# Another formula for the booked time of a TensorE product, in the planner that places the side work of a two-layer block

## The chip, the cores and the metric

The kernel runs on one core of a Trainium2 chip. A core has TensorE (matrix products, PE in the profile, with its weight loads as PEld), VectorE (DVE), ScalarE (ACT), GpSimd (POOL) and the queue engine SyncE (SP). Each engine runs its instructions in the order in which the program lists them and waits where an input or a buffer is not ready. The metric is the time of one execution on the device, in microseconds.

## The reference

Two layers, each on 256 latent tokens `x` and 256 context tokens `ctx` of width 1024. Cut to what matters:

```
h = rmsnorm(x, norm_w) * (1 + scale) + shift          # scale, shift, gate from w_ada; the same for ctx
parts = split_cols(h @ w_in)                          # 13 parts, 13328 columns
A: h_a = mlstm(q, k, v, gates), 4 heads, two directions; context first, then x
   y_a = rmsnorm(h_a) * sigmoid(o) * silu(z)
B: differential attention, 8 heads with two maps each; q and k normalised over 64 features, rotated
   y_b = rmsnorm(o_b) * (1 - lam_init) * silu(z)
C: y_c = real(fft2(u)) * silu(z), 4 groups of 256 features
y = sum over A, B, C of sigmoid(m) * (y_i @ w_i_out)
x = x + gate * (y @ w_out)                            # ctx likewise, except in the last layer
```

All values are 32-bit floats. The result is `x` after both layers.

## The kernel before

Every matrix product of two 32-bit operands is made of three TensorE products of a rounded part and its remainder (`hi*hi`, `hi*lo`, `lo*hi`; `three` in the code). The normalised input stands feature-major in `hTh` (rounded) and `hTl` (remainder), 8 blocks of 128 features by 512 tokens.

The main stream goes through the columns of all weights in pieces of 512 rows by 256 columns (272 where the gate columns of branch A ride along). For each piece SyncE's queue loads `raw` (4 buffers), ScalarE casts it to `wh` and VectorE subtracts to get `wl` (3 buffers each), and TensorE multiplies. `next_piece` asks `prefetch` to emit these steps three pieces ahead. A chunk of 256 columns uses two pieces; its result stands in one of three PSUM banks `pm` and is drained by ScalarE and VectorE. The order of the chunks is a list per layer: `A0 A1 ... W0` (heads of A, pairs of heads of B, groups of C, merges M, output W).

All else is side work, written as generators: the gates of branch A (`gates_side`), the scores and weighted sums of a head of A (`a_side`), the softmax of B, the transforms of C, the columns of `w_ada`, and the norm of the next layer (`next_norm`, four units, each four transposes on TensorE, two `ntmp` on ScalarE, two on VectorE, the cast `hTh` on ScalarE and the remainder `hTl` on VectorE). They use five further PSUM banks `ps`. Between two main products `tick` lets the side generators take a step. When a step is due is decided by the planner while the program is written: `Clocks` keeps an estimated time for each engine, every instruction adds a booked duration to its engine's clock (`mm` and `transpose` for TensorE, `Paced` for the others), and starts no earlier than the booked ends of what it reads. A generator yields the time at which its next step may go, mostly `when(...)`: the booked end of its inputs plus 400 ns. `tick` takes the step once TensorE's clock has passed that time, at most 500 ns of TensorE's work at once, and only while the clocks of VectorE and ScalarE are less than 1500 ns ahead of TensorE's (4000 in W). The whole order on every engine comes out of these booked numbers.

Names for what follows. In branch A, `acol` and `ecol` hold per-token gate values, `dR` gate values in memory; `a_side` loads them back, spread over 128 partitions, as `Rb` (a DMA that GpSimd issues, 448 KB in layer 1), forms four score blocks, copies them to `S`, runs four `Rb` relus with `acol` and an exponential, and multiplies. `to` and `Ga` are the output gates of a head. `vt`, `qkh`, `Q`, `K`, `sq`, `bst` belong to branch B: `bst` are sums of squares (VectorE), raised to a power by GpSimd (two instructions each). In the second layer the first head of A does its gates first and then finishes whatever is left of the norm units:

```
            if l and h == 0:
                yield from oz()
                drain(normers)
```

The functions that book TensorE's time and what takes the steps:

Of the kernel before, what the change touches and what calls it, by code (L numbers as in the profile page):

```python
# [10 lines left out]
F32 = mybir.dt.float32  # L11
# [39 lines left out]
def a_parts(d, stream):  # L51
    """(source token tile, first query token, queries, offset) of each position of direction d"""
    o = S_ORDER[d]
    if stream == 0:
        return [(o[0], 0, 256, 0), (o[1], 128 * o[1], 128, 256)]
    return [(o[0], 256, 256, 0), (o[1], 256, 256, 256), (o[2], 256, 256, 512), (o[3], 128 * o[3], 128, 768)]
# [34 lines left out]
class Clocks:  # L91
    """When each engine gets to what is emitted, estimated, to place the side work among the main products."""

# [4 lines left out]
    def book(self, engine, outs, ins, cost, tail):  # L98
        """an instruction of engine: names of tiles written and read, time held, time until the result is seen"""
        start = self.t[engine]  # L100
        for n in outs + ins:
            e, at = self.wrote.get(n, (engine, 0.0))
            if e != engine:
                start = max(start, at)
        for n in outs:
            for e, at in self.read.get(n, {}).items():
                if e != engine:
                    start = max(start, at)
        self.t[engine] = end = start + cost
        for n in ins:  # L110
            self.read.setdefault(n, {})[engine] = end + SEM_NS
        for n in outs:
            self.wrote[n] = (engine, end + tail + SEM_NS)
        return end

    def rotate(self, tag, bufs, name):
        """the tile called name takes the place of the one bufs before it"""
        r = self.ring.setdefault(tag, [])
        r.append(name)
        if len(r) > bufs:  # L120
            self.read[name] = {"": self.last(r[-1 - bufs])}
# [5 lines left out]
class Paced:  # L127
    """An engine whose instructions are booked as they are emitted."""

# [37 lines left out]
def hybrid_kernel(ctx: ExitStack, tc: tile.TileContext, t):  # L167
    nc = tc.nc
    x_in, ctx_in, out = t["x"], t["ctx"], t["out"]
    est = Clocks()  # L170
# [15 lines left out]
    def when(*tiles, banks=1):  # L186
        """the time at which the tiles are written and side banks are free"""
        r = est.ring.get("ps", [])
        old = r[-SIDEB:][:banks] if len(r) >= SIDEB else []
        return max([0.0] + [est.wrote[v.name][1] for v in tiles if v.name in est.wrote] + [est.last(n) for n in old]) + READY_NS  # L190
# [14 lines left out]
    def gen_pair(shape, name):  # L205
        """hi and lo parts, in one slot where they fit"""
        if 8 * int(np.prod(shape[1:])) <= 4128:
            p = gen([shape[0], 2] + shape[1:], F32R, name)
            return p[:, 0], p[:, 1]
        return gen(shape, F32R, name), gen(shape, F32R, name)  # L210
# [17 lines left out]
    def mm(o, a, b, start, stop):  # L228
        n = int(np.prod(b.shape[1:]))
        ins = [v.name for v in (a, b) if v.name not in ("hTh", "hTl")]  # L230
        est.book("pe", [o.name], ins, max(n * 0.4167 + 2.5, 27) * (4 if b.dtype == F32 else 1) / (128 // o.shape[0]), 160)
        nc.tensor.matmul(out=o, lhsT=a, rhs=b, start=start, stop=stop)  # L232

    def transpose(o, a, idn):
        est.book("pe", [o.name], [a.name], 112, 160)
        nc.tensor.transpose(o, a, idn)  # L236
# [8 lines left out]

    # ------------------------------------------------------------- constants
    xt = {}
# [72 lines left out]
    def rstd_of(ss, n, shape):  # L320
        """(ss / n + eps) ** -0.5 on GpSimd, in place; returns the time at which it is done"""
        gpsimd.tensor_scalar(ss, ss, 1.0 / n, EPS, op0=ALU.mult, op1=ALU.add)
        gpsimd.tensor_tensor(ss, ss, chalf.to_broadcast(shape), op=ALU.pow)
        return when(ss)

    # ------------------------------------------------------------- per-layer small parameters
    def load_params(l):
# [35 lines left out]

    # ------------------------------------------------------------- adaLN
    def ada_bias(l, piece):
        """b_ada of 1024 columns in the first two rows of a tile of zeros"""
        brow = gen([128, 1024], F32, "brow")
        gpsimd.memset(brow, 0.0)
        gpsimd.dma_start(out=brow[0:2, :],
                            in_=t["b_ada"][l:l + 1, 512 * piece:512 * piece + 1024].to_broadcast([2, 1024]))  # L370
        return brow

    def ada_rows(l, piece, dma):
        """w_ada of 512 columns"""
        raws = []
# [7 lines left out]
    def ada_mm(raws, brow, dst):  # L383
        """sc @ w_ada + b_ada: partitions 32 g + stream hold four partial sums"""
        ps = ps_side()
        for k in range(KT):
            g = k % 4
# [10 lines left out]
    def ada_finish(l, pc, ks=slice(0, 8)):  # L398
        """pc: shift and scale of some blocks of features"""
        if l not in abt:  # L400
# [8 lines left out]
    def ada_gen(l, pieces):  # L409
        """shift and scale columns (pieces 0..3) as a side generator"""  # L410
        acc = small([128, 32], "adac", 1)
# [32 lines left out]

    # ------------------------------------------------------------- norm -> feature-major h
    hTh = const.tile([128, KT, 512], F32R, tag="hTh", name="hTh")
    hTl = const.tile([128, KT, 512], F32R, tag="hTl", name="hTl")

    def norm_stats(tiles):
        """normalized copies of some token tiles"""  # L450
        outs, sums = [], []
# [9 lines left out]
    def norm_apply(l, i, src, base):  # L461
        """src: the normalized transposed blocks base .. base + 3 of token tile i; returns the closing step"""
        ab = abt[l]
# [21 lines left out]

    # ------------------------------------------------------------- weight pieces
    plan = []
# [57 lines left out]
    def wcols(w, *cols, form=None):  # L545
        """two pieces of some columns; even features before odd ones along the columns or in pairs of row blocks"""
        srcs = [(w[:, c:c + n], n) for c, n in cols]
        plan.append((0, srcs, form))
        plan.append((1, srcs, form))

    # ------------------------------------------------------------- main-stream products
    def three(o, a, b, first, last):
# [8 lines left out]
    def fm_chunk(rhs, evac, ntok, bank=ps_main, step=4):  # L561
        """two 128-column blocks of W, feature-major: out[block][128 cols, tokens]"""
        if isinstance(ntok, int):
# [23 lines left out]
    def tm_chunk(lhs, tiles, evac, single=False, step=4):  # L587
        """256 columns of W, token-major: out[pair][128 tokens, 2, 256]"""
        n = 1 if single else 2
# [22 lines left out]

    # ------------------------------------------------------------- side machinery
    side = []
# [38 lines left out]

    # ============================================================= one layer
    def layer(l, P):
# [8 lines left out]
        def packed(name, i):  # L664
            """[128, 2, NTOK], two of them in a slot where they fit"""
            if NTOK == 512:
# [4 lines left out]

        # ---------- branch A: gates
        def gates_side():
            """kind x head i of the gate preactivations: from column 32 x + i, token-major, to a partition"""
            yield when(gpad)
# [69 lines left out]

        # ---------- branch A: heads
        def a_proj(h):
# [178 lines left out]

        # ---------- branch B
        def b_proj(g):
# [57 lines left out]
        def b_side(g):  # L986
# [37 lines left out]
            def softmax(hd, i, p2, n):  # L1024
                """the weighted difference of both maps, short of the first one's 1 / sum"""
                c0 = 4 * i + 2 * hd
# [89 lines left out]

        # ---------- branch C
        def c_proj(g):
# [3 lines left out]
            def evu(a, pr, ps):  # L1122
                """sums and differences of features d and d + 128"""
                F = gen([128, 2, 384], F32, "fold")
# [62 lines left out]

        # ---------- merge
        yacc = {}

        def merge(recs, ahead, key, first, final):
# [6 lines left out]
            def spread(g, every):  # L1198
                """split a y that is there after each so many steps"""
                for n, _ in enumerate(g):  # L1200
# [83 lines left out]

    # ============================================================= program
    def plan_layer(l):
# [32 lines left out]

    # ---- start: the first products follow the adaLN columns, a quarter of the features at a time  # L1320
    raws = {}
# [32 lines left out]
    def turn(q, hold=False):  # L1354
        """x, feature-major"""
        xT[q] = gen([128, 2, 512], F32, "xT")
# [12 lines left out]
    def quarter(q):  # L1369
        """the scale and shift of a quarter of the features, and what they make of x"""  # L1370
        ps = ps_side()
# [124 lines left out]
```

## Time and profile before

| what | us |
|---|---|
| median of 3 runs | 1522.9 |
| the runs | 1522.81 to 1523.61 |
| span of the profiled execution | 1521.1 |
| TensorE busy in it | 1499.1 |
| VectorE busy | 971.5 |
| ScalarE busy | 735.0 |
| GpSimd busy | 145.7 |

The profile was taken from one execution whose span, from its first to its last instruction, is 1521.1 us; the median of the runs is 1.8 us longer. The granted TensorE clock is 1.000 of full speed over the whole span. In the stretch table the columns are the stretch, its length, then for each engine the busy time and the count of instructions. In a timeline a row is start, duration, engine, line, operation, what is written and read, shape, and in brackets how long the engine was idle just before and what ended that.

### The profile page before, as it was taken

The numbers are of one execution on the slowest core, as the hardware profiler recorded it, in microseconds if no ns is written. First come the engines' busy times: TensorE is split into PE (matmuls) and PEld (weight loads), VectorE is DVE, ScalarE is ACT, GpSimd is POOL, SyncE is SP. The second block draws the span as 40 slices with busy tenths as digits, with TensorE's granted clock in tenths as the row PEclk, the third lists the DMA queues.
The fourth block names the chain that finished last, engine by engine and source line by source line (L and its number), as shares of the span: only waits on it lengthen the run. The fifth ranks groups of instructions, "written<-read, shape, count | busy, mean of one in ns | idle before, by whom it ended". The sixth has DMA issues, their size and how long they took to land.

```text
span 1521.1 us, 25867 instructions
## 1 busy us (share of the span) xinstructions
PE 1499.1 (99%) x10410; PEld 1350.8 (89%) x10410; DVE 971.5 (64%) x1833; ACT 735.0 (48%) x1384; POOL 145.7 (10%) x193
## 2 busy tenths in 40 slices
PE   6999999999999999999999999999999999999999
PEld 4888889999998987897786789999999999999998
DVE  3447666677677586436664367677687666977765
ACT  4443556544544545334432235545557554656443
POOL 4001000020100010001024001001020011000200
PEclk9999999999999999999999999999999999999999
DMA  9524333332222222223249337544344523545754
GB/s 310 167 84 127 87 94 105 105 97 70 75 67 69 70 84 70 84 84 97 70 144 337 78 112 228 139 131 133 115 111 118 167 84 109 169 139 153 256 162 151
DMA packets 181611, 192.07 MB, mean 126 GB/s; under 512 B 9818, under 2 KB 174612, under 8 KB 181492
## 3 DMA queue, kind: packets, MB, share of 16 engines
q1 hardware_dynamic: 170080, 159.93, 35.6%
q0 software_dynamic: 7936, 27.27, 5.9%
q10 hardware_dynamic: 3476, 3.23, 0.7%
q8 instruction: 81, 1.33, 0.4%
q14 instruction: 38, 0.31, 0.1%
HBM read 188.23 MB, written 2.17 MB: 125 GB/s over the span
## 4 chain that ended last, share of the span: by engine, by line
PE 92%; DVE 3%; SPq 2%; issue 1%; ACT 1%; DMA 1%; ACTq 0%; DVEq 0%
PE pm L232 76%; PE ps L232 13%; PE ps L236 3%; SPq L161 2%; DVE wl L161 1%; DVE Rx L161 1%; DMA raw<-in_w_in_dram 0%; DVE Rc L161 0%; DMA prow<-in_a_norm_w_dram 0%; DVE lfm L161 0%; DVE at L161 0%; ACT lse L161 0%; DVE Ga L161 0%; ACT wh L161 0%; DVE ntmp L161 0%
## 5 line engine op out<-in xcount | busy, mean ns | idle before, releaser
L161 DVE TENSOR_TENSOR wl<-raw,wh 128x1024 fp32r<-128x1024 f32 x280 | 340.9, 1223 | 193.4 <-ACT wh L161 192.8
L161 ACT CAST wh<-raw 128x1024 fp32r<-128x1024 f32 x280 | 293.6, 1054 | 169.0 <-PE pm L232 135.0
L232 PE MATMUL pm<-hTh,wh 128*128 128x256 f32 (+1 forms) x1008 | 349.0, 346 | 0.0
L232 PE MATMUL pm<-hTl,wh 128*128 128x256 f32 (+1 forms) x1008 | 342.8, 340 | 0.0
L232 PE MATMUL pm<-hTh,wl 128*128 128x256 f32 (+1 forms) x1008 | 342.4, 340 | 0.0
L232 PE MATMUL pm<-wh,hTh 128*128 128x256 f32 (+1 forms) x1152 | 329.8, 286 | 1.5 <-DVE Ga L161 0.8
L232 PE MATMUL pm<-wl,hTh 128*128 128x256 f32 (+1 forms) x1152 | 324.1, 281 | 0.7 <-DVE wl L161 0.7
L232 PE MATMUL pm<-wh,hTl 128*128 128x256 f32 (+1 forms) x1152 | 324.2, 281 | 0.3 <-DVE hTl L161 0.2
L232 PEld LDWEIGHTS pm<-wh,hTh 128*128 128x128 f32 x1152 | 217.3, 189 | 10.4 <-issue 5.5
L232 PEld LDWEIGHTS pm<-wl,hTh 128*128 128x128 f32 x1152 | 216.9, 188 | 2.1 <-DVE wl L161 1.0
L232 PEld LDWEIGHTS pm<-wh,hTl 128*128 128x128 f32 x1152 | 217.5, 189 | 0.7 <-DVE hTl L161 0.7
L232 PEld LDWEIGHTS pm<-hTh,wh 128*128 128x128 f32 x1008 | 189.7, 188 | 30.8 <-issue 9.9
L232 PEld LDWEIGHTS pm<-hTh,wl 128*128 128x128 f32 x1008 | 189.5, 188 | 23.3
L232 PEld LDWEIGHTS pm<-hTl,wh 128*128 128x128 f32 x1008 | 189.7, 188 | 19.0
L232 PE MATMUL pm<-y,wh 128*128 128x512 f32 (+1 forms) x768 | 192.7, 342 | 0.0
L232 PEld LDWEIGHTS pm<-y,wh 128*128 128x128 f32 x768 | 128.9, 188 | 18.3 <-issue 2.6
L232 PE MATMUL pm<-y,wl 128*128 128x512 f32 (+1 forms) x384 | 129.4, 337 | 0.0
L161 ACT ACTIVATE Pt<-ps,mx,qsc 128x512 f32<-128x512 f32 (+1 forms) x96 | 67.1, 706 | 27.7 <-DVE mx L161 22.0
L232 PEld LDWEIGHTS pm<-y,wl 128*128 128x128 f32 x384 | 72.2, 188 | 8.6
L232 PE MATMUL pm<-wh,yf 128*128 128x256 f32 x384 | 73.0, 287 | 0.0
L232 PEld LDWEIGHTS pm<-wh,yf 128*128 128x128 f32 x384 | 59.9, 188 | 0.3
L161 DVE TENSOR_REDUCE mx<-ps 128x1 f32<-128x512 f32 (+1 forms) x96 | 53.0, 593 | 4.3 <-PE ps L232 4.2
(243 smaller groups left out, 1969.8 us busy)
## 6 DMA issues: line engine op xcount, KB each, us to landing
raw<-in_w_in_dram SPq DMA_DIRECT2D x192, 512.0 KB, 3.7
adaw<-in_w_ada_dram POOLq DMA_DIRECT2D x32, 512.0 KB, 7.1
raw<-in_w_out_dram SPq DMA_DIRECT2D x24, 512.0 KB, 4.5
adaw<-in_w_ada_dram SPq DMA_DIRECT2D x16, 512.0 KB, 8.5
raw<-in_w_in_dram SPq DMA_DIRECT2D x32, 256.0 KB, 3.3
raw<-in_w_a_out_dram SPq DMA_DIRECT2D x16, 512.0 KB, 3.4
raw<-in_w_c_out_dram SPq DMA_DIRECT2D x32, 256.0 KB, 3.4
raw<-in_w_b_out_dram SPq DMA_DIRECT2D x16, 512.0 KB, 3.8
```

The source lines that it names most:

```text
L161: return f(*a, **k)
L232: nc.tensor.matmul(out=o, lhsT=a, rhs=b, start=start, stop=stop)
L236: nc.tensor.transpose(o, a, idn)
```

## The change

In `mm` the booked time of a product is another formula. Before it was columns x 0.4167 + 2.5 ns, at least 27, four times that for plain 32-bit products, divided by 128 / rows of the result as a whole number. Now it is columns x 0.4453 + 4 ns, four times that for plain 32-bit products, at least 105, times the rows of the result over 128 and the rows of the operands over 128. A product of 256 columns was booked at 109.2 ns and is now booked at 118.0, one of 512 at 215.9 and now 232.0, one of 128 at 55.8 and now 105. A transpose was booked at 112 and is now at 109. All other lines of the diff blank a comment or a docstring.

```diff
     def mm(o, a, b, start, stop):
         n = int(np.prod(b.shape[1:]))
         ins = [v.name for v in (a, b) if v.name not in ("hTh", "hTl")]
-        est.book("pe", [o.name], ins, max(n * 0.4167 + 2.5, 27) * (4 if b.dtype == F32 else 1) / (128 // o.shape[0]), 160)
+        est.book("pe", [o.name], ins, max((n * 0.4453 + 4) * (4 if b.dtype == F32 else 1), 105) * o.shape[0] / 128 * a.shape[0] / 128, 160)
         nc.tensor.matmul(out=o, lhsT=a, rhs=b, start=start, stop=stop)
 
     def transpose(o, a, idn):
-        est.book("pe", [o.name], [a.name], 112, 160)
+        est.book("pe", [o.name], [a.name], 109, 160)
         nc.tensor.transpose(o, a, idn)
```

The instructions are the same on every engine; their order differs from about the 40th microsecond on. Three places follow, first as it was, then as it is. A row is the line that emits, the operation, what is written and read (numbers tell buffers apart), the shape, and the engines or queues it waits for.

ScalarE at the boundary of the layers: the last three and a half norm units, the cast of a weight piece, the gates of the first head of layer 1. Before:

```order
L161 CAST hTh<-ntmp_9433 128x4x128 [waits DVE_49,Activation_49]
L161 ACTIVATE ntmp_9447<-ps_9442,ab_8298 128x128 [waits PE_49]
L161 ACTIVATE ntmp_9447<-ps_9442,ab_8298 128x128
L161 CAST hTh<-ntmp_9447 128x4x128 [waits DVE_49,Activation_49]
L161 CAST wh_9456<-raw_9323 128x1088 [waits DMAHW5_49,DMAHW4_49]
L161 ACTIVATE ntmp_9468<-ps_9463,ab_8298 128x128 [waits PE_49]
L161 ACTIVATE ntmp_9468<-ps_9463,ab_8298 128x128
L161 CAST hTh<-ntmp_9468 128x4x128 [waits DVE_49,Activation_49]
L161 ACTIVATE ntmp_9483<-ps_9478,ab_8298 128x128 [waits PE_49]
L161 ACTIVATE ntmp_9483<-ps_9478,ab_8298 128x128
L161 CAST hTh<-ntmp_9483 128x4x128 [waits DVE_49,Activation_49]
L161 ACTIVATE Ga_9320<-pm_9399 128x256 [waits PE_49]
```

Now:

```order
L161 CAST hTh<-ntmp_9427 128x4x128 [waits DVE_49,Activation_49]
L161 ACTIVATE ntmp_9441<-ps_9436,ab_8267 128x128 [waits PE_49]
L161 ACTIVATE ntmp_9441<-ps_9436,ab_8267 128x128
L161 CAST hTh<-ntmp_9441 128x4x128 [waits DVE_49,Activation_49]
L161 ACTIVATE ntmp_9456<-ps_9451,ab_8267 128x128 [waits PE_49]
L161 ACTIVATE ntmp_9456<-ps_9451,ab_8267 128x128
L161 CAST hTh<-ntmp_9456 128x4x128 [waits DVE_49,Activation_49]
L161 ACTIVATE ntmp_9471<-ps_9466,ab_8267 128x128 [waits PE_49]
L161 ACTIVATE ntmp_9471<-ps_9466,ab_8267 128x128
L161 CAST hTh<-ntmp_9471 128x4x128 [waits DVE_49,Activation_49]
L161 CAST wh_9480<-raw_9323 128x1088 [waits DMAHW5_49,DMAHW4_49]
L161 ACTIVATE Ga_9320<-pm_9399 128x256 [waits PE_49]
```

The weight cast from `raw_9323` stood in the middle of the units and stands behind the last of them; `Ga` follows in both.

ScalarE in the first head of layer 1, from the cast of a weight piece to the first relus of `Rb`. Before:

```order
L161 CAST wh_10002<-raw_9789 128x4x256 [waits DMAHW1_49,DVE_49,PE_49]
L161 CAST vt_9924<-pm_9932 128x2x128 [waits PE_49]
L161 CAST vt_9925<-pm_9932 128x2x128 [waits DVE_49]
L161 ACT_TABLE_LOAD
L161 ACTIVATE ecol_10044<-ps_10051 128x32 [waits PE_49]
L161 COPY S_10062<-ps_10064 128x256 [waits PE_49]
L161 COPY S_10062<-ps_10069 128x256 [waits PE_49]
L161 COPY S_10062<-ps_10077 128x256 [waits PE_49]
L161 COPY S_10062<-ps_10083 128x256 [waits PE_49]
L161 ACTIVATE Rb_10060<-Rb_10060,acol_10043 128x256 [waits DMASW3_49,DVE_49]
```

Now:

```order
L161 CAST wh_10002<-raw_9789 128x4x256 [waits DMAHW1_49,DVE_49,PE_49]
L161 ACT_TABLE_LOAD
L161 ACTIVATE ecol_10022<-ps_10029 128x32 [waits PE_49]
L161 COPY S_10040<-ps_10042 128x256 [waits PE_49]
L161 COPY S_10040<-ps_10047 128x256 [waits PE_49]
L161 COPY S_10040<-ps_10055 128x256 [waits PE_49]
L161 COPY S_10040<-ps_10061 128x256 [waits PE_49]
L161 CAST vt_9924<-pm_9932 128x2x128 [waits PE_49]
L161 CAST vt_9925<-pm_9932 128x2x128 [waits DVE_49]
L161 ACTIVATE Rb_10038<-Rb_10038,acol_10021 128x256 [waits DMASW3_49]
```

The two casts to `vt` (values of branch B) stood ahead of the table load, `ecol` and the four copies `S`, and stand behind them.

ScalarE in the second A head of layer 1. Before:

```order
L161 COPY S_10588<-ps_10590 128x256 [waits PE_49]
L161 CAST wh_10607<-raw_10484 128x4x256 [waits DMAHW5_49,DVE_49,PE_49]
L161 ACTIVATE Ga_9320<-pm_10553 128x256 [waits PE_49]
L161 ACTIVATE Ga_9320<-pm_10553 128x256 [waits DVE_49]
L161 CAST wh_10650<-raw_10521 128x4x256 [waits DMAHW6_49,Activation_49]
L161 CAST wh_10681<-raw_10554 128x4x256 [waits DMAHW7_49,PE_49,Activation_49]
L161 COPY Q_10646<-pm_10654 128x512 [waits PE_49]
L161 CAST wh_10715<-raw_10605 128x4x256 [waits DMAHW0_49,Activation_49]
L161 COPY S_10588<-ps_10769 128x256 [waits PE_49]
L161 COPY S_10588<-ps_10774 128x256 [waits PE_49]
L161 COPY S_10588<-ps_10783 128x256 [waits PE_49]
L161 ACTIVATE Rb_10586<-Rb_10586,acol_10043 128x256 [waits DMASW5_49]
```

Now:

```order
L161 CAST wh_10594<-raw_10481 128x4x256 [waits DMAHW5_49,DVE_49,PE_49]
L161 COPY S_10618<-ps_10620 128x256 [waits PE_49]
L161 COPY S_10618<-ps_10625 128x256 [waits PE_49]
L161 COPY S_10618<-ps_10633 128x256 [waits PE_49]
L161 COPY S_10618<-ps_10639 128x256 [waits PE_49]
L161 ACTIVATE Rb_10616<-Rb_10616,acol_10021 128x256 [waits DMASW5_49]
L161 ACTIVATE Rb_10616<-Rb_10616,acol_10021 128x256 x2
L161 ACTIVATE Rb_10616<-Rb_10616,acol_10021 128x128
L161 ACTIVATE Ga_9320<-pm_10552 128x256 [waits PE_49]
L161 ACTIVATE Ga_9320<-pm_10552 128x256 [waits DVE_49]
L161 CAST wh_10666<-raw_10513 128x4x256 [waits DMAHW6_49,Activation_49]
L161 CAST wh_10697<-raw_10553 128x4x256 [waits DMAHW7_49,PE_49,Activation_49]
```

The four copies `S` and the four relus of `Rb` stood behind `Ga`, three weight casts and `Q`, with only one `S` ahead; all of them now stand ahead of `Ga` and of the casts from `raw_10513` and `raw_10553`.

VectorE at the same place: the two reductions to `bst` that GpSimd's powers follow. GpSimd's own order (both powers, then the DMA of `Rb`) is the same. Before:

```order
L161 TENSOR_REDUCE bst_10457<-sq_10458 128x16
L161 SCALAR_TENSOR_TENSOR qkl_10182<-pm_10336,qkh_10181 128x512 [waits Activation_49]
L161 TENSOR_TENSOR wl_10487<-raw_10253,wh_10486 128x4x256 [waits DMAHW2_49,PE_49,Activation_49]
L161 TENSOR_SCALAR H_10092<-H_10092,hs_10430 128x256 [waits Pool_49]
L161 TENSOR_SCALAR H_10092<-H_10092,hs_10430 128x256
L161 TENSOR_REDUCE bst_10457<-sq_10516 128x8 [waits Activation_49]
L161 TENSOR_TENSOR wl_10524<-raw_10317,wh_10523 128x4x256 [waits DMAHW3_49,PE_49,Activation_49]
L161 TENSOR_TENSOR wl_10557<-raw_10401,wh_10556 128x4x256 [waits DMAHW4_49,PE_49,Activation_49]
```

Now:

```order
L161 TENSOR_TENSOR wl_10516<-raw_10321,wh_10515 128x4x256 [waits DMAHW3_49,PE_49,Activation_49]
L161 TENSOR_REDUCE bst_10471<-sq_10472 128x16
L161 SCALAR_TENSOR_TENSOR Ga_9320<-ps_10546,awcol_106,Ga_9320 128x256 [waits PE_49]
L161 TENSOR_TENSOR wl_10556<-raw_10384,wh_10555 128x4x256 [waits DMAHW4_49,Activation_49]
L161 SCALAR_TENSOR_TENSOR Ga_9320<-ps_10571,awcol_106,Ga_9320 128x256 [waits PE_49]
L161 TENSOR_REDUCE bst_10471<-sq_10578 128x8 [waits Activation_49]
L161 TENSOR_TENSOR wl_10595<-raw_10481,wh_10594 128x4x256 [waits DMAHW5_49,PE_49,Activation_49]
```

The reduction of 16 columns stood ahead of three weight pieces (`wl_10487`, `wl_10524`, `wl_10557`) and now stands behind the second of these; the one of 8 columns stood behind one of them and now stands behind all three.

## Rows read from the trace of the kernel before

**Rows 1.** The page's head and its first section: busy time, share, count.

```profile
span 1521.1 us, 25867 instructions
...
PE 1499.1 (99%) x10410; PEld 1350.8 (89%) x10410; DVE 971.5 (64%) x1833; ACT 735.0 (48%) x1384; POOL 145.7 (10%) x193
```

**Rows 2.** Busy time by stretch: PE, PEld, DVE, ACT, POOL, clock, DMA.

```profile
40.00:900.00 860.00, 859.23 (x5182) 737.04 (x5182) 512.39 (x990) 387.55 (x744) 76.43 (x93) 1.00 0.35 102
900.00:1000.00 100.00, 98.47 (x776) 95.86 (x775) 67.25 (x99) 54.11 (x90) 8.31 (x16) 1.00 0.57 170
1000.00:1100.00 100.00, 98.58 (x807) 96.42 (x805) 73.22 (x162) 51.72 (x93) 9.77 (x12) 1.00 0.45 130
1100.00:1400.00 300.00, 300.00 (x2458) 289.62 (x2458) 227.38 (x432) 173.09 (x340) 26.52 (x28) 1.00 0.45 130
```

**Rows 3.** TensorE's waits: us in total, times, longest.

```profile
PE ps L232 <- ACT ecol L161: 1.4, 1, 1.4
...
PE pm L232 <- DVE Ga L161: 0.8, 1, 0.8
...
PE pm L232 <- DVE wl L161: 0.7, 1, 0.7
```

**Rows 4.** The chain that ended last, 880 to 920 us: start, length, what.

```profile
904.07 5.67 PE pm L232 x48
```

**Rows 5.** Timeline of TensorE, 967 to 977 us.

```profile
968.67 0.29 PE L232 MATMUL pm<-wh,hTh 128*128 128x272 f32 x1
969.70 0.39 PE L232 MATMUL pm<-wl,hTh 128*128 128x272 f32 x1 [0.74 <-DVE wl L161]
...
974.09 0.29 PE L232 MATMUL pm<-wh,hTl 128*128 128x272 f32 x1
975.16 0.39 PE L232 MATMUL pm<-wh,hTh 128*128 128x272 f32 x1 [0.79 <-DVE Ga L161]
```

**Rows 6.** Timeline of ScalarE, 960 to 975 us.

```profile
962.86 0.81 ACT L161 ACTIVATE ntmp<-ps,ab 128x128 f32<-128x128 f32 x2 [1.27 <-PE ps L236]
...
965.04 0.81 ACT L161 ACTIVATE ntmp<-ps,ab 128x128 f32<-128x128 f32 x2
...
967.23 1.10 ACT L161 CAST wh<-raw 128x1088 fp32r<-128x1088 f32 x1
```

**Rows 7.** Timeline of VectorE, 966 to 976 us.

```profile
968.36 1.29 DVE L161 TENSOR_TENSOR wl<-raw,wh 128x1088 fp32r<-128x1088 f32 x1 [1.15 <-ACT wh L161]
```

**Rows 8.** Timeline of TensorE, 1016 to 1024 us.

```profile
1019.27 0.28 PE L232 MATMUL ps<-qkh,qkl 128*128 128x256 f32 x1
1020.97 0.38 PE L232 MATMUL ps<-qkh 128*128 128x256 f32 x1 [1.42 <-ACT ecol L161]
```

**Rows 9.** Timeline of ScalarE, 1013 to 1027 us.

```profile
1019.03 0.37 ACT L161 CAST vt<-pm 128x256 fp32r<-128x256 f32 x1 [2.74 <-DVE vt L161]
1019.42 1.28 ACT L161 ACT_TABLE_LOAD   x1
```

**Rows 10.** Timeline of ScalarE, 1058 to 1082 us.

```profile
1065.30 0.39 ACT L161 ACTIVATE Ga<-pm 128x256 f32<-128x256 f32 x1 [1.91 <-PE pm L232]
...
1066.97 2.23 ACT L161 CAST wh<-raw 128x1024 fp32r<-128x1024 f32 x2
...
1077.26 1.60 ACT L161 ACTIVATE Rb<-Rb,acol 128x256 f32<-128x256 f32 x4
```

**Rows 11.** Timeline of VectorE, 1049 to 1068 us.

```profile
1057.04 0.68 DVE L161 TENSOR_REDUCE bst<-sq 128x8 f32<-128x512 f32 x1
...
1060.43 1.23 DVE L161 TENSOR_TENSOR wl<-raw,wh 128x1024 fp32r<-128x1024 f32 x1 [1.58 <-ACT wh L161]
1061.57 0.87 DVE L161 SCALAR_TENSOR_TENSOR Ga<-ps,awcol,Ga 128x256 f32<-128x256 f32 x2
```

**Rows 12.** Timeline of GpSimd, 1045 to 1066 us.

```profile
1058.23 0.68 POOL L161 TENSOR_SCALAR bst<-bst 128x8 f32<-128x8 f32 x1
...
1060.57 1.18 POOL L161 DMA_DIRECT2D Rb<-dR  x2
```

**Rows 13.** The instructions on `Rb`: its 24 loads, issue and landing.

```profile
L161 POOL DMA_DIRECT2D Rb<-dR x24: 536/546/624, 134.9 to 1190.8; - x24
...
DMA to landing us min/median/max: 3.5/4.5/7.2
```

## The prediction

> **What bounds the kernel now.** I read the page first: of a span of 1521.1 us TensorE is busy for 1499.1 [rows 1]. Then the busy times by stretch, to see where the other 22.0 us lie [rows 2]: 0.77 us between 40 and 900 us, 1.53 between 900 and 1000, 1.42 between 1000 and 1100, nothing between 1100 and 1400. So 3.7 us of idle time lie in these stretches, and the remaining 18.3 us lie in the first 40 us, where the change leaves every engine's order as it was, and in the last 121 us. TensorE bounds the kernel nearly everywhere, by its product count, which the change does not touch: in a quiet part 48 main products take 5.67 us, that is one start every 118 ns, on the chain of waits itself [rows 4]. The list of what TensorE waited for names the little that can be won: 1.4 us for `ecol` (ScalarE), 0.8 for `Ga` and 0.7 for `wl` (VectorE), once each [rows 3]. Against that stands all that can be lost, since VectorE, ScalarE and GpSimd run in the order of emission and feed TensorE.
>
> **What the change does to the planner.** The old formula books a main product of 256 columns at 256 x 0.4167 + 2.5 = 109.2 ns, the new one at 256 x 0.4453 + 4 = 118.0 ns. The rows say 118. The new number is the true one; but until now TensorE ran some 8% slower than booked, so that a step placed "when its data are ready" really had 8% more time for them. With the new booking the planner's TensorE clock passes each due time after fewer products, so side steps come earlier in the product stream. The bookings of VectorE, ScalarE and GpSimd are the old ones. Where these were short of the truth, the hidden reserve is what covered it. No busy time is added anywhere; the cost lies in which wait falls where. I followed both orders and looked for places where what TensorE needs moves behind something that is late. Three matter.
>
> **Term 1, the boundary of the layers (loss).** In the order before, ScalarE casts the weight piece `wh_9456` between the second and the third of the last four norm units (two `ntmp`, one `hTh`); now all four units stand ahead of the cast, and on VectorE its `wl` stands behind the third `hTl` instead of the first. One unit takes 965.04 - 962.86 = 2.18 us [rows 6], a chain over two engines that nothing shortens. The first unit's transposes now stand 15 instead of 21 products behind the start of their chunk, 6 x 0.118 = 0.7 us earlier. So the units begin near 962.2 and end at 962.2 + 4 x 2.18 = 970.9; the cast (1.10 [rows 6]) ends at 972.0, the subtraction (1.29 [rows 7]) at 973.3, and with a tenth for the handover TensorE goes on at 973.45. Today it goes on at 969.70 after its product at 968.67 [rows 5]: a new wait of 3.75 us on top of the present one. Part comes back. From 969.70 to 974.09 TensorE has 4.39 us of products, and then stands until 975.16 for `Ga` [rows 5]. From 973.45 those products end at 977.85, and `Ga` needs 973.3 plus two ScalarE and four VectorE pieces, some 2.4 us, so it is done near 975.9 and waits for nobody. The product that starts at 975.16 now starts at 977.9: **+2.75 us**. The bounds: if nothing of `Ga` comes back +3.75; if the units close up to 1.6 us each, when ScalarE does the next unit's `ntmp` while VectorE holds the one before, 4 x 0.55 = 2.2 less, +0.5. I take 2.75, since today's first two units, between which nothing stands, take 2.18.
>
> **Term 2, the scores of head A0 in layer 1 (gain).** The fourth score product waits today from 1019.39 to 1020.97 [rows 8], 1.57 us, for the PSUM bank that `ecol` has to read. `ecol` is late since ScalarE sat 2.74 us ahead of a `vt` that waits for VectorE, then loaded a function table for 1.28 us [rows 9]. Now the table load and `ecol` stand ahead of both `vt`, so the 1.28 us pass while ScalarE has nothing else. TensorE gets there some 18 products, 2.1 us, earlier in the stream; the gate chain on VectorE ahead of it starts earlier by fewer steps, by my estimate from the two orders 1.1 to 1.4 us; and the bank waited for is now that of `acol` on VectorE, so about 0.35 us of wait stay: **-1.2 us**, bounds -1.57 (no wait left) and 0 (all of it comes back as a wait for `acol`).
>
> **Term 3, the second A head of layer 1 (loss).** Take T = 1065.30, where the last chunk ahead of it ends and ScalarE starts `Ga` [rows 10]. Before, one score copy `S` stood ahead of T, and the other three with the four `Rb` relus came two pieces after the next `Ga` and casts, at 1077.26 with no wait [rows 10]. Now all four `S` and all four `Rb` stand ahead of `Ga`, and behind `Ga` stands the cast of the piece that TensorE needs next but two. `Rb` must have been loaded by a DMA that GpSimd issues behind two powers of `bst`, and in VectorE's order the reductions feeding these now stand behind one or two weight pieces more. I work it forward: the `wl` ahead of the second reduction runs from 1060.43 to 1061.57, one `Ga` (0.87 / 2) and the reduction (0.68) bring 1062.7 [rows 11]; GpSimd takes from there what it takes today from 1058.23 to the DMA at 1060.57, 2.34 us [rows 12], so the DMA is issued near T - 0.2. It lands 3.5 to 7.2 us later, 4.5 in the median [rows 13]: T + 4.3. Four relus, 1.60: T + 5.9. `Ga` on ScalarE, VectorE, ScalarE, three times 0.4: T + 7.1. The cast, 2.23 / 2 [rows 10]: T + 8.2. The subtraction, 1.23, and a handover: T + 9.5. TensorE has two pieces of 24 products in store, 48 x 0.118 = 5.7, and needs the low part a product later, T + 5.8. It stands for **+3.7 us**. Nothing later gives that back, for TensorE is the bound from there to 1400 us. Bounds: 0, if the planner's early steps leave GpSimd's chain much earlier than I placed it, and +6.4 with the longest landing of 7.2. I take the median landing.
>
> The Trainium skill, "DMA: Bandwidth & Descriptors", section on the anatomy of one DMA on the GpSimd path, puts a transfer at about 2.0 us plus its bytes at 436 GB/s; for these 448 KB that is an estimate of 3.05 us. The 24 loads of this trace contradict it: not one landed in under 3.5 us [rows 13]. By the page term 3 would be 1.45 us smaller, near +2.25; I stay with the rows.
>
> **Term 4, small ones.** Around 1290 us two weight pieces stand behind a few more `kT`, `qT`, `sq` and `Gb` steps, with little reserve. I put **+0.3 us**, bounds 0 and +1 (one piece's subtraction, 1.2 us [rows 11], late by most of itself). The other moves I cost at nothing: they are covered by the three pieces of weights in store, 2.8 us of products each; without that cover each would cost about one cast, 1.1 us.
>
> **Sum.** 2.75 - 1.2 + 3.7 + 0.3 = +5.55 us. On the profiled span of 1521.1 that gives 1526.65; the runs shown have a median of 1522.9, 1.8 us above that span, so the forecast is 1528.5 us. All low ends together (0.5 - 1.57 + 0 + 0) give -1.1, or 1521.8; all high ends (3.75 + 0 + 6.4 + 1) give +11.2, or 1534.
>
> **Rivals.**
> First, the other side: the booking now matches the rows (118.0 against 118), so each side step comes when its data are there, the three waits of [rows 3] go, and nothing takes their place. That is worth 1.57 + 0.9 + 0.95 = 3.4 us: 1519.5. For it speaks that those waits exist and that one of them is undone in the order. Against it stand the two other orders. It decides at the layer boundary: `wl` would have to be done at 968.8, so the four norm units would have to take (968.8 - 2.4 - 962.2) / 4 = 1.05 us each, half of the 2.18 they take. And `Rb` would have to land within 1 us of its issue, against 3.5 at the least.
> Second, no change: the products are the same, TensorE is 99% busy, and the pieces in store hide what moves. If term 3 falls away (GpSimd's chain early enough), 2.75 - 1.2 + 0.3 = +1.85 stay, 1524.7; if both losses are half as large as I have them, +2.3, 1525.2. If term 1 alone falls away, +2.8, 1525.7. For it speaks that beyond 1100 us there is no idle time at all, so there reserves are large [rows 2]. Against it, that the delays are sums of measured durations with no free parameter but the landing.
> Third, a larger loss: the reserve of 8% goes everywhere, and what I count at two places happens at each of the A and B heads of the second layer, four and four. With two further waits of the size of term 3, +5.55 + 7.4 = +13, 1536. For it speaks that the bookings of the other engines and of the loads stayed as they were, so whatever is booked too short there now meets a stream without reserve; against it, that the orders show no third place with a load standing ahead of a weight cast.
>
> **How the numbers follow.** A measurement of this kernel can tell about 0.2%, 3.0 us, from no change: below 1519.9 is faster, above 1525.9 slower. My forecast, with losses between +3 and +10, has 0.68; the larger loss 0.05; no change, in its three forms, 0.19; the other side 0.08. So slower 0.73, same 0.19, faster 0.08. The range from 1521.5 to 1533 goes from the case where only the low ends hold to near the sum of the high ends, and leaves out the other side and the larger loss, with some 0.15 to 0.2 together.
>
> **What would show it.** Term 1: in the timeline of TensorE a wait of about 4.6 us for `wl` at the first products of 272 columns, and no wait for `Ga` behind it. Term 2: the wait for `ecol` gone or under 0.4 us, perhaps named `acol`. Term 3: a wait for `wl` of 3 to 5 us near 1075 us, with ScalarE idle some 4 us ahead of `Rb`, released by a DMA. I am wrong if the norm units go through in 1.6 us or less, if `Rb` is there when the last `S` has been copied, or if the list of TensorE's waits beyond 40 us stays under 4 us in all.

## The result: 1537.2 us, slower, and outside the range

The changed kernel takes 1537.19 us in the median of its runs (1536.89 to 1541.61), the kernel before 1523.23: a ratio of 1.0096, interval 1.0082 to 1.0110. Slower was forecast, at 1528.5 with a range up to 1533; the loss is 14.0 us where 5.6 were worked out.

The head of the page after, and the stretches that answer to [rows 2] (busy time of PE, PEld, DVE, ACT, POOL, then the granted clock):

```profile
span 1539.8 us, 25846 instructions
...
PE 1509.2 (98%) x10410; PEld 1357.9 (88%) x10410; DVE 971.4 (63%) x1833; ACT 735.5 (48%) x1384; POOL 148.0 (10%) x193
```

```profile
0.00:40.00 40.00, 25.36 (x189) 17.64 (x190) 13.62 (x33) 16.54 (x29) 16.28 (x32) 0.96 1.02 317
40.00:900.00 860.00, 859.67 (x5196) 737.71 (x5196) 511.74 (x990) 387.08 (x744) 77.86 (x93) 1.00 0.34 101
900.00:1000.00 100.00, 95.52 (x719) 92.07 (x718) 63.61 (x94) 49.65 (x84) 8.35 (x16) 0.97 0.58 170
1000.00:1100.00 100.00, 94.40 (x747) 92.38 (x747) 69.04 (x145) 49.29 (x85) 10.03 (x12) 0.97 0.42 125
1100.00:1400.00 300.00, 298.22 (x2425) 285.59 (x2424) 225.08 (x442) 171.27 (x348) 26.86 (x28) 1.00 0.41 120
```

Two things are to be seen. TensorE is idle in the two stretches that the prediction named: 4.5 us against 1.5 and 5.6 against 1.4. And TensorE is busier, 1509.2 us against 1499.1 [rows 1], with the same products: in those stretches the granted clock is 0.97 and no longer 1.00. The slow products counted below make up 4.9 of these 10 us; the rest is not traced. (This one execution, 1541.6 us, is 4.4 us above the median; its clock was also at 0.96 in the first 40 us. A second profile, below, has 1.00 there.)

What TensorE waited for, answering to [rows 3]:

```profile
PE pm L232 <- ACT wh L161: 6.7, 2, 3.5
...
PE pm L232 <- DVE wl L161: 2.7, 4, 0.9
...
PE ps L236 <- DVE at L161: 0.9, 2, 0.6
...
PE ps L232 <- DVE acol L161: 0.6, 1, 0.6
```

`ecol` and `Ga` have left the list; `wh`, for which TensorE never waited, leads it with two waits. Both in TensorE's timeline, with the products behind them. At the boundary of the layers ([rows 5] before):

```profile
971.59 0.29 PE L232 MATMUL pm<-wh,hTl 128*128 128x272 f32 x1
975.07 0.59 PE L232 MATMUL pm<-wh,hTh 128*128 128x272 f32 x1 [3.20 <-ACT wh L161]
976.40 0.59 PE L232 MATMUL pm<-wl,hTh 128*128 128x272 f32 x1 [0.73 <-DVE wl L161]
976.79 0.43 PE L232 MATMUL pm<-wh,hTl 128*128 128x272 f32 x1
977.02 0.43 PE L232 MATMUL pm<-wh,hTh 128*128 128x272 f32 x1
...
981.10 0.35 PE L232 MATMUL pm<-wh,hTh 128*128 128x272 f32 x1
981.28 0.29 PE L232 MATMUL pm<-wl,hTh 128*128 128x272 f32 x1
981.41 0.29 PE L232 MATMUL pm<-wh,hTl 128*128 128x272 f32 x1
```

And in the second A head of layer 1:

```profile
1079.45 0.28 PE L232 MATMUL pm<-wh,hTl 128*128 128x256 f32 x1
1083.26 0.38 PE L232 MATMUL pm<-wh,hTh 128*128 128x256 f32 x1 [3.53 <-ACT wh L161]
1084.52 0.58 PE L232 MATMUL pm<-wl,hTh 128*128 128x256 f32 x1 [0.88 <-DVE wl L161]
1084.90 0.42 PE L232 MATMUL pm<-wh,hTl 128*128 128x256 f32 x1
1085.12 0.41 PE L232 MATMUL pm<-wh,hTh 128*128 128x256 f32 x1
...
1090.45 0.28 PE L232 MATMUL pm<-wl,hTh 128*128 128x256 f32 x1
```

Read the starts, not the durations. Ahead of the first wait the products of 272 columns start 126 ns apart (981.41 - 981.28 is 0.13 as well); behind it 977.02 - 976.79 = 0.23. The same at 1085.12 - 1084.90 = 0.22 against 0.118 for 256 columns [rows 4]. The granted clock of those stretches, two microseconds each:

```profile
976.00:978.00 2.00, 1.60 (x7) 1.60 (x8) 1.97 (x5) 0.69 (x4) 0.00 (x0) 0.50 0.25 31
...
982.00:984.00 2.00, 2.00 (x18) 2.00 (x17) 0.35 (x1) 0.37 (x1) 0.00 (x0) 1.00 0.59 207
```

It is 0.50, TensorE's lower level of 1.2 GHz, until about 981.1 and 1090.4, and 1.00 (2.4 GHz) thereafter. The products between 976.40 and 981.10 lose about 2.2 us by it; the 27 between 1084.52 and 1090.45 take 5.93 us instead of 27 x 0.118 = 3.19, a loss of 2.7.

Why `wh` was late is as the prediction had it. ScalarE at the boundary: the four units, then the cast, ending near 975.0:

```profile
965.18 0.81 ACT L161 ACTIVATE ntmp<-ps,ab 128x128 f32<-128x128 f32 x2 [0.56 <-PE ps L236]
...
967.38 0.80 ACT L161 ACTIVATE ntmp<-ps,ab 128x128 f32<-128x128 f32 x2
...
973.92 1.09 ACT L161 CAST wh<-raw 128x1088 fp32r<-128x1088 f32 x1
```

One unit takes 967.38 - 965.18 = 2.20 us, and four of them 8.74 (2.18 and 8.72 were put in). In the second head ScalarE stands for `Rb`'s load with `Ga` and the cast queued behind it:

```profile
1079.54 1.60 ACT L161 ACTIVATE Rb<-Rb,acol 128x256 f32<-128x256 f32 x4 [5.43 <-DMA Rb<-dR]
1081.04 0.36 ACT L161 ACTIVATE Ga<-pm 128x256 f32<-128x256 f32 x1
...
1082.17 1.98 ACT L161 CAST wh<-raw 128x1024 fp32r<-128x1024 f32 x2
```

GpSimd issued that load at this row, 5.8 us before the relus could start:

```profile
1073.76 1.18 POOL L161 DMA_DIRECT2D Rb<-dR  x2
```

### The profile page after: what moved, and what is told of

It reads as the page before. It is cut to its first block, busy times and chain, and to the rows that moved or that the text cites. A ratio compares the mean times of both kernels' runs of the same rounds, so it can differ in the third digit from the quotient of the medians.

```text
span 1539.8 us, 25846 instructions
## 1 busy us (share of the span) xinstructions
PE 1509.2 (98%) x10410; PEld 1357.9 (88%) x10410; DVE 971.4 (63%) x1833; ACT 735.5 (48%) x1384; POOL 148.0 (10%) x193
## 4 chain that ended last, share of the span: by engine, by line
PE 90%; DVE 4%; ACT 2%; issue 1%; DMA 1%; POOL 1%; ACTq 0%; POOLq 0%; DVEq 0%
PE pm L232 74%; PE ps L232 13%; PE ps L236 3%; DVE wl L161 1%; DMA Rb<-dR 1%; DVE Rx L161 1%; ACT wh L161 1%; DMA crow<-in_c_dram 0%; POOL bst L161 0%; DVE Rc L161 0%; ACT ntmp L161 0%; ACT hTh L161 0%; ACT junk L161 0%; POOL nss L161 0%; DVE at L161 0%
```

## Experiments

**The two places, one at a time.** The first edit holds the third norm unit until the second weight piece of the values is split (the lines that fill `second_v` are left out here), the second lets the relus of `Rb` in the second layer wait for the load's booked landing, the third is both.

```diff
                 for b in range(2):
+                    while i == 1 and b == 0 and emitted["split"] <= second_v[0]:
+                        yield after(50)
                     f = norm_apply(1, i, transpose_half(xs[i], b), 4 * b)
```

```diff
                     Rn[ui + 1] = load_R(*units[ui + 1])
+                if last:
+                    yield when(R)
                 for st, t0, w, o in parts:
```

> The changed kernel, but the third norm unit at the layer boundary waits in the planner until the second weight piece of the values has been split, so that the cast stands in the middle of the units again, as before the change. Theory (a wait above some length also lowers TensorE's granted clock, which then costs more than the wait): the 4.6 us of waits near 971 to 976 us shrink to the 1.9 us of before (2.75 us won) and the 23 products of 272 columns that started 227 ns apart there start 126 ns apart again (2.3 us won), clock 1.00 between 960 and 1000 us: about 1532.1 us against 1537.2. Rival (the waits alone cost, the low clock comes from elsewhere and stays): about 1534.4 us. Second rival (the place costs nothing in the end, later work had slack): 1537.

Measured: 1532.33 us (1531.74 to 1533.70), 4.9 below the changed kernel.

> The changed kernel, but in the second layer the relus of an A head's Rb wait in the planner for the booked landing of their load, so that they no longer stand ahead of Ga and of two weight casts. Theory: the 4.8 us of waits near 1079 to 1085 us go, and with them the 27 products that started 213 ns apart instead of 118 (2.6 us): about 1530 us against 1537.2, clock 1.00 between 1050 and 1100 us. Rival (waits alone): about 1532.4 us. Second rival (the load is late in any order and the wait appears at the relus' new place): 1536 to 1537.

Measured: 1530.65 us (1529.09 to 1531.83), 6.5 below.

> The changed kernel with both edits, norm units and relus. Theory: the two gains add, 5.05 and 7.4 us: about 1525 us, the clock at 1.00 from 40 us on, and the 2 to 4 us that remain above the kernel before lie behind 1100 us, in small waits for wl and for the operands of branch C. Rival (waits alone): 1529.6 us. Rival (the reserve is gone everywhere, and removing two waits makes others longer): above 1531 us.

Measured: 1524.39 us (1522.91 to 1526.25), 12.8 below; against the kernel before 1.0006, interval 0.9996 to 1.0015.

The stretches 960 to 1000 and 1050 to 1100 us, with the norm units held:

```profile
960.00:1000.00 40.00, 39.17 (x302) 37.64 (x301) 23.95 (x36) 22.41 (x43) 0.54 (x1) 1.00 0.41 119
1050.00:1100.00 50.00, 46.44 (x357) 45.14 (x356) 34.25 (x76) 24.72 (x43) 7.74 (x8) 0.93 0.43 124
```

with the relus held:

```profile
960.00:1000.00 40.00, 35.99 (x252) 34.38 (x251) 20.56 (x32) 17.81 (x38) 0.55 (x1) 0.91 0.38 109
1050.00:1100.00 50.00, 50.00 (x405) 48.23 (x404) 37.52 (x78) 27.56 (x49) 7.02 (x8) 1.00 0.46 135
```

and with both, where neither stretch shows a lower clock:

```profile
960.00:1000.00 40.00, 39.17 (x302) 37.65 (x301) 23.81 (x36) 23.02 (x43) 1.07 (x2) 1.00 0.43 125
1050.00:1100.00 50.00, 50.00 (x408) 48.36 (x407) 37.75 (x78) 27.11 (x50) 7.02 (x8) 1.00 0.47 135
```

The low clock goes with its wait and only with it. All three times lie within 0.7 us of the theory that counts the slow products (1532.1, 1530, 1525) and 1.8 to 5.2 us below the one that counts waits alone (1534.4, 1532.4, 1529.6). The two places make up 12.8 of the 14.0 us that were lost.

**What a wait of known length costs.** In the kernel before, away from all of this, VectorE multiplies two rows of a weight remainder in use by 1.0 (the lines that choose the eight places are left out here):

```diff
+            for _ in range(stalls.pop(0)):
+                nc.vector.tensor_scalar(wl[:, 1:3, :], f32(wl[:, 1:3, :]), 1.0, None, op0=ALU.mult)
```

> The kernel before with eight waits put into the merges of layer 0: VectorE multiplies two rows of a wl piece in use by 1.0 in place, 1, 2, 3, 4, 5, 6, 8 and 10 times in a row, after TensorE has read the one row and before it reads the other. At about 0.5 us each the waits go from some 0.5 to 5 us. Theory (the clock falls only after a wait of some 3 us or more, as at 971 and 1079 us of the changed kernel, and not after the 0.9 to 1.7 us of the kernel before): the short ones leave products at their distance, behind the long ones they start at nearly twice the distance for 5 to 6 us, so that each long one costs 2 to 3 us more than its length. Rival (the low clock has to do with what ran before, not with the length of the wait): no fall here, or falls without order.

Measured: 1561.81 us, the median of two runs (1560.58 and 1563.04). In all TensorE waited for the eight:

```profile
PE pm L232 <- DVE wl L569: 26.9, 8, 5.7
```

The fourth and the sixth, in the timeline, with how long TensorE was idle:

```profile
645.40 0.50 PE L232 MATMUL pm<-y,wl 128*128 128x512 f32 x1 [2.75 <-DVE wl L569]
...
737.20 0.79 PE L232 MATMUL pm<-hTh,wl 128*128 128x512 f32 x1 [3.67 <-DVE wl L569]
```

and the granted clock behind the fourth, fifth and sixth (behind the last two it reads 0.51 and 0.50):

```profile
645.40:651.40 6.00, 6.00 (x30) 5.03 (x31) 2.62 (x4) 1.05 (x1) 0.00 (x0) 1.00 0.21 72
707.20:712.00 4.80, 4.77 (x11) 3.81 (x12) 3.55 (x5) 0.00 (x0) 0.00 (x0) 0.50 0.00 0
737.20:742.00 4.80, 4.80 (x14) 3.36 (x15) 1.19 (x5) 0.00 (x0) 0.00 (x0) 0.50 0.09 30
```

The four shorter ones, up to 2.75 us idle, left the clock at 1.00; all four from 3.67 us on brought it to 0.50.

The products of TensorE run in the same order as in the kernel before, so each start can be set against its counterpart. The product behind the fifth wait and the last one ahead of the sixth, first in the kernel before:

```profile
693.36 0.39 PE L232 MATMUL pm<-hTh,wl 128*128 128x512 f32 x1
...
717.00 0.40 PE L232 MATMUL pm<-hTl,wh 128*128 128x512 f32 x1
```

and with the waits:

```profile
707.23 0.80 PE L232 MATMUL pm<-hTh,wl 128*128 128x512 f32 x1 [4.36 <-DVE wl L569]
...
733.13 0.40 PE L232 MATMUL pm<-hTl,wh 128*128 128x512 f32 x1
```

The first of the two starts 707.23 - 693.36 = 13.87 us later than its counterpart, the second 733.13 - 717.00 = 16.13: between them the low clock cost 2.26 us. In the same way it is 2.6, 2.2 and 2.4 us behind the other three long waits, and 0.1 us behind each short one. So a fall costs about 2.4 us here, on top of its wait. The long waits all came last, so this run alone does not part length from place; but the waits of 3.20 and 3.53 us in the changed kernel, at other places, brought the clock down as well. That is what the prediction lacked, measured by itself. The Trainium skill, "TensorE: Matmul & The Clock Gate", part 1 on the clock gate, says that the clock falls to 1.2 GHz after idleness and comes back after a time of work; the rows above agree (0.50 behind 3.67 us of idle time; 1.00 again at 982 us in the changed kernel, with TensorE at work). It should have stood among the rivals.

**Which half of the formula.** First the cost per column alone (n x 0.4453 + 4), then all the rest (floor 105, both row factors, 109 for a transpose).

> The kernel before with one part of the change alone: a product costs columns x 0.4453 + 4 ns in the planner (118.0 for 256 columns); the floor, the factor for rows and the booking of a transpose stay old. Both bad places then stand in the order as in the changed kernel. Theory (the 8% on main products alone moves the side work, and the two long waits with the low clock behind them make up the loss): within 2 us of the changed kernel's 1537.2. Rival (the small products, booked twice and half as much, share the blame): 1525 to 1532.

Measured: 1538.44 us (1535.86 to 1540.33). The 8% on a main product suffice for the two waits: TensorE is idle there for 3.18 us ahead of the product at 974.03 and for 2.19 ahead of the one at 1080.27, each time with a second wait (0.94 and 0.88 us) one product later, and the clock falls behind both.

> The other part alone: the floor of 105 ns, the factors for rows of the result and of the operands and 109 ns per transpose are the new ones, while a product costs columns x 0.4167 + 2.5 ns as before (109.2 for 256 columns). The layer boundary and the second A head of layer 1 stand in the order as before. Theory: 1523 to 1525, no wait above 2 us, clock 1.00 from 40 us on. Rival (small products matter): 1528 or more.

Measured: 1538.26 us (1537.67 to 1538.69). A miss: as expected there is no long wait and a full clock from 900 to 1400 us, but 14 us are lost in one place later on, which neither the kernel before nor the changed one has:

```profile
1418.44 0.38 PE L232 MATMUL ps<-vt,W 128*128 128x256 f32 x1 [0.82 <-ACT W L161]
...
1432.11 1.09 PE L236 MATMUL ps<-first,Q 128*128 128x128 f32 x4 [3.47 <-DVE Q L161]
```

Where the merge of branch B begins, `drain(recs)` emits whatever the last B softmax has left, with no main products in between. Counted while the program is written, that is 3 steps in the kernel before, 0 in the changed one, 12 here; no trace shows this count. The clock falls here too:

```profile
1422.00:1427.00 5.00, 3.83 (x14) 2.85 (x14) 1.65 (x3) 1.24 (x4) 0.00 (x0) 0.50 0.00 0
```

To test that reading, the same kernel with the planner's limit on VectorE and ScalarE loosened for the end of layer 1, so that 0 steps are left:

```diff
-        backlog[0] = BACKLOGW if kind == "W" else (BACKLOG0, BACKLOG1)[l]
+        backlog[0] = BACKLOGW if kind == "W" else 4000.0 if l and (kind, i) in (("C", 2), ("C", 3), ("M", 1)) else (BACKLOG0, BACKLOG1)[l]
```

> The small-product half of the change alone, as in the run that lost 14 us near 1417 to 1432 us, but VectorE and ScalarE may be booked 4000 instead of 1500 ns ahead of TensorE from the third group of branch C to the merge of branch B in layer 1. In that run 12 steps of the last B softmax were still to do when that merge began, and were emitted in one go (3 in the kernel before, none in the changed one); now none are. Theory (the 14 us are this one place: TensorE waits step by step for a softmax emitted in one go, with the low clock behind it): 1523 to 1525. Rival (the softmax cannot be had earlier, the waits only move ahead of the merge): above 1530.

Measured: 1525.31 us (1523.93 to 1527.43): 13 us are gone; of the 2.4 that remain above the kernel before, 2.0 are two new waits of 1.24 and 0.75 us near 1437. So the half with the small products is harmless at the two places, and its own loss was the steps left for the merge.

**Giving the reserve back.** The changed kernel with VectorE's and ScalarE's bookings times 1.08.

> The changed kernel with the bookings of VectorE and ScalarE raised by 8% as well, so that the ratio of the bookings is about the old one. At the layer boundary the weight cast stands in the middle of the units again, and Rb's relus no longer stand ahead of Ga. Theory (what was lost is the reserve between TensorE's booking and the others'): 1523 to 1526, no wait above 2 us. Rival (any order that the new number makes is worse): above 1530.

Measured: 1546.23 us (1545.70 to 1547.00). The theory falls as it was put. The two places are cured (TensorE is busy for 50.00 of the 50 us from 1050 on), but 24 steps of the last softmax are left for the merge, and between 1414 and 1442 TensorE waits for `W` and `Q` and runs at the low clock, as in the run with the small products; the loss is 23 us in all. One ratio of bookings does not make an order good; each order has its own weak places.

**A search for a version faster than both.** Two edits to the kernel before: norm units two to four held behind the first head's output gates, scores of that head held behind `ecol`.

> The kernel before with its own booking and two holds in the planner: at the layer boundary the second to fourth norm units are emitted only behind the output gates of the first head (so that weight cast and Ga come first), and the scores of the first A head of layer 1 wait for the booked end of ecol plus 1.6 us. Theory (waits below 3 us cost just their length): the waits of 0.9, 0.95 and 1.57 us go, 3.4 us in all, 1519.9 against 1523.3. Rival (the units, now later, make the products of the third and fourth token tile wait, or the value tiles' banks): 1522 to 1525.

Measured: 1529.86 us (1529.00 to 1530.51). The wait for `ecol` went, but a new one of 1.4 us for `gpad` took most of the gain at the boundary, and 6 steps were left for the merge, with a wait of 3.5 us for `Q` and a clock of 0.97 from 1400 us on.

> The kernel before with its own booking, the scores of the first A head of layer 1 held behind ecol, the third and fourth norm unit held behind the output gates, and the 4000 ns of above for the end of layer 1, so that the last B softmax is done ahead of its merge. Theory (each of the waits of 0.95 and 1.57 us goes, nothing takes their place): about 1521, at best 1520.5, against 1523.3. Rival (a new order always finds a new wait): 1523 or more.

Measured: 1524.23 us (1523.82 to 1525.34), 1.0008 of the kernel before, interval 1.0000 to 1.0017. Between 900 and 1100 us TensorE is idle for 1.17 us where it was for 2.95, a gain of 1.8; between 1100 and 1440 us, where it was never idle, it now is for 2.0. No version of these beats the kernel before; the best ones equal it.

**The changed kernel once more.**

> The changed kernel once more, unchanged, for a profile of another execution: 1537 us, and not the 1541.6 of the first profile, whose clock was at 0.96 in the first 40 us; the waits near 971 and 1079 us and the low clock behind both are to stand in it as in the first.

Measured: 1536.73 us (1535.92 to 1540.79), a profile with clock 1.00 in the first 40 us. The second place in it:

```profile
1080.11 0.38 PE L232 MATMUL pm<-wh,hTh 128*128 128x256 f32 x1 [2.50 <-ACT wh L161]
1081.37 0.39 PE L232 MATMUL pm<-wl,hTh 128*128 128x256 f32 x1 [0.88 <-DVE wl L161]
1081.59 0.28 PE L232 MATMUL pm<-wh,hTl 128*128 128x256 f32 x1
1081.71 0.28 PE L232 MATMUL pm<-wh,hTh 128*128 128x256 f32 x1
1081.83 0.36 PE L232 MATMUL pm<-wl,hTh 128*128 128x256 f32 x1
1081.99 0.42 PE L232 MATMUL pm<-wh,hTl 128*128 128x256 f32 x1
1082.21 0.42 PE L232 MATMUL pm<-wh,hTh 128*128 128x256 f32 x1
```

Idle for 2.50 us and, one product later, for 0.88 us, TensorE still runs three products at full distance, and then the clock falls while it is busy. Here it is back at full distance from about 1085.3 on, so that the fall costs 1.5 us. The product ahead of these rows starts at 1077.33; the waits come to (1080.11 - 1077.33) + (1081.37 - 1080.11) - 2 x 0.12 = 3.80 us.

## Why the prediction was wrong

*Order and places: right.* All three places that the prediction read from the orders moved as it said, and the two losses stand where it put them.

*Term 1, +2.75 of waiting: right, and only half of the price.* TensorE stood (975.07 - 971.59) + (976.40 - 975.07) - 2 x 0.126 = 4.56 us, against 1.85 before [rows 5]: +2.71. "About 4.6 us, and no wait for `Ga` behind it" is what the timeline shows, save that most of it is named `wh`. What was missing are the 2.2 us of slow products. Undoing the place won 4.9.

*Term 3, +3.7 of waiting: right, same fault.* 3.80 us in the second profile, 4.83 in the first; from the load's issue to the relus it took 4.8 us in the one and 5.8 in the other (1076.39 - 1071.63, 1079.54 - 1073.76). To this come 2.7 us of slow products in the first profile and 1.5 in the second. Undoing it won 6.5. The 4.5 us taken for the load is the median of all 24 [rows 13]; the 16 of them that move 448 KB, as this one does, have 5.3 in the same trace, the 8 of 192 KB have 4.0. The estimate of 3.05 us by the Trainium skill, "DMA: Bandwidth & Descriptors", section on the anatomy of one DMA on the GpSimd path, is too short for this load; the measurement decides.

*The step that failed* is thus the one by which each wait was priced: "a new wait of 3.75 us", "it stands for +3.7 us", with every product behind it taken at the 118 ns of [rows 4]. That distance belongs to a clock of 1.00, which was seen over the whole trace of a kernel that, once past its start, never stood longer than 1.6 us. The change made waits longer than any in that trace, so the row could not be carried over. With 2.4 us for each fall, as the run with the eight waits prices it, the same sum gives 5.55 + 4.8 = +10.35, or 1533.3. That is about half of what was missing; the rest lies in terms 2 and 4 and in what is not assigned.

*Term 2, -1.2: the mechanism right, the size too good.* The wait for `ecol` (1.42 us idle) is gone, but waits for `acol` (0.57) and for `at` (0.63) stand in its place, so about -0.2. The lower reserve was named as a bound, at 0.

*Term 4, +0.3: too small.* From 1100 to 1400 us TensorE is now idle for 1.78 us, before for none, and a wait of 0.56 us near 948 is new. That is 2.3 us in several small waits (2.1 in the second profile), the "reserve that goes everywhere" of the third rival, at a third of the size given there. By the second profile, where the slow products at the boundary lose 2.5 us, the terms are 2.7 + 2.5 - 0.2 + 3.8 + 1.5 + 2.1 = 12.4 of 1535.4 - 1521.1 = 14.3 us; some 2 us are not assigned.

*The rivals.* The other side (accurate booking, no new wait) did not come, though the waits for `ecol` and `Ga` did go. What no rival saw is that the changed order leaves no softmax step for the merge of branch B, a place at which three other orders lost some 7 to 23 us. The larger loss named 1536, close to what was measured, but by luck: its two further waits of the size of term 3 did not come.

## What to carry to other kernels

Ask of every wait that a change makes whether it is longer than any that the trace before shows: a duration per product is only good for the clock at which it was read, and a fall to the lower level here cost 1.5 to 2.7 us on top of its wait. In a stream planned by booked times a truer number is no better order; look for the few places where a cast that TensorE needs is queued behind a load or a chain, and for what a drain has to emit in one go. Moving such a place repairs it, but rearranges all that follows.

## What the runs showed of the hardware

The clock did not fall for the made waits of up to 2.75 us idle and fell for all four from 3.67 us on. It also fell at waits of 2.69 us (norm units held), 2.50 (second profile of the changed kernel) and 2.19 (cost per column alone), each with a second wait of 0.88 us one product later; in the second profile three products ran at full distance ahead of the fall. A pair of 1.24 and 0.75 us (small products, limit loosened) left it at 1.00. By these few cases a wait is not to be judged alone: what stands close to it seems to count too. The first 40 us had a clock of 0.96 in one profiled execution of the changed kernel and 1.00 in another.
